# One gemv unit ahead of the last mean matmuls and four or five behind, at three entries of a two-block transformer kernel

## The chip, the core and the metric

The kernel runs on one core of a Trainium2 chip. The metric is the device time of one execution in microseconds, as the median of several runs. One execution was also profiled; rows below are from its trace. PE is TensorE's matmul side and PEld its weight loads, DVE is VectorE, ACT ScalarE, POOL GpSimd and SP the engine whose queue issues the weight transfers.

## What is computed

Two transformer blocks over one sequence of 256 tokens, 1024 channels wide, in float32. The first block has two layers, each with a mixer and a SwiGLU FFN; between them one key/value product is made from the residual stream:

```
h = x
for layer in range(2):
    sh1, sc1, g1, sh2, sc2, g2 = split(silu(c) @ mod_w[layer] + mod_b[layer], 6)
    u = rms_norm(h, norm_mix) * (1 + sc1) + sh1
    h = h + g1 * (hgrn2(u) if layer == 0 else band_attention(u, k, v))
    u = rms_norm(h, norm_ffn) * (1 + sc2) + sh2
    h = h + g2 * swiglu(u, ffn_w_in, ffn_w_out)
    if layer == 0:
        shift, scale = split(silu(c) @ kv_mod_w + kv_mod_b, 2)
        k, v = split((rms_norm(h, kv_norm) * (1 + scale) + shift) @ kv_w, 2)
x = rms_norm(h, final_norm)
```

The second block has four kinds of attention side by side and a convolutional FFN; the diff does not touch its code.

## The kernel before

Activations lie transposed (channels on partitions). Every product in full precision is made of three fp32r matmuls (mm3, lines 258 to 260): weights and activations are each split into a rounded high part and a low remainder. A weight arrives as a *unit* of 512 KB: `emit_dma` (L186) loads it into one of 7 raw buffers (RAW_BUFS), `emit_conv` casts it on ACT (w_hi, L193) and subtracts on DVE (w_lo, L195) into one of 4 pairs of buffers. A raw buffer is free again when its unit has been converted.

The modulation vectors are products of one row with a matrix (gemv). Their units are *raw*: not converted, but multiplied in float32 straight from the raw buffer, on PE with the row as weights (L524) or on DVE by multiply and add (L516, L518). A raw buffer of such a unit is free when the engine has read it. `gemv` has 8 units; `gemv_x` does the first 5 (NF) on PE and the rest on DVE.

The program is a list of steps, and the instructions are emitted step by step, for all engines, in that order. Before each step `pump` emits what may be emitted of transfers and conversions: the transfer of unit i if unit i-7 has been consumed in an earlier step, and the conversion of the next weight unit j if at most 2 (AHEAD) converted units lie ahead and `j <= state["pos"] + state["look"]`, where pos is the number of units that the steps so far have taken, raw ones included. look is 4 (LOOK) from the first projections on.

There are three *entries* where a product begins on a freshly normalized residual: the FFN of layer 0 (stA), the key/value product (stB) and the FFN of layer 1 (stC). The product before each (the last step of an output projection or of an FFN) works on four banks of 512 columns; after each bank DVE adds into the residual (L623), ACT squares (L428) and PE sums the squares with a matrix of constants (`stat_mm`, L463), each time one bank or more behind. `barrier` lays out the rest: gemv units in `fill`, and in a step f between them the last mean matmul, ACT's logarithm and exponential (L468, L469) and `apply_parts`: for each of 8 channel groups a scaled product on DVE (nt, L573), the high part on ACT (s, L579) and the low part on DVE (s, L585). The next product's first matmul needs the first high part. For stB and stC, fill is the first 5 units of a gemv_x product (g12, g15). For stA it is part of the 8 units of the sixth modulation product of layer 0 (g05), all on PE; three of these 8 stand ahead of the last step of the output projection (`aproj[6:]`, which takes two weight units).

Of the kernel before, what the change touches and what calls it, by code (L numbers as in the profile page):

```python
# [27 lines left out]
NF = 5  # L28
NG = 6
LOOK = 4  # L30
NB = 2
RAW_BUFS = 7
WT_BUFS = 4
AHEAD = 2
# [14 lines left out]
HG_ORDER = """  # L49
# [82 lines left out]
def kernel(ctx: ExitStack, tc: tile.TileContext, x, c, mod_w, mod_b, norm_mix, norm_ffn,  # L132
# [28 lines left out]
    def open_phase(name):  # L161
        if "cm" in phase:
            phase["cm"].__exit__(None, None, None)
        phase["cm"] = tc.tile_pool(name=name, bufs=2, reuse_waits="tile")
        phase["p"] = phase["cm"].__enter__()

    def ph(w, name, bufs=2, dt=F32, tag=None):
        return phase["p"].tile([P, w], dt, name=name, tag=tag or name, bufs=bufs)
# [9 lines left out]
    state = {"pos": 0, "dma": 0, "conv": 0, "conv_w": 0, "used_w": 0, "look": -1, "late": None}  # L178
# [123 lines left out]
    def out_proj(w, ks, operand, evac, nlast=2):  # L302
        box = {}

        def first(i, u):
            if i == 0:
                box["a"] = [acc_bank() for _ in range(4)]
            hi, lo = operand(ks[i])
            acc_pairs(box["a"], u, hi, lo, range(4), i == 0, False)

        n0 = len(ks) - nlast

        def last(*us):
            for j in range(4):
                for i, u in enumerate(us, n0):
                    hi, lo = operand(ks[i])
                    acc_pairs(box["a"], u, hi, lo, [j], False, i == len(ks) - 1)
                evac(j, box["a"][j])

        st = [Step(lambda u, i=i: first(i, u), [unit_row(w, P * ks[i])], 2.6) for i in range(n0)]  # L320
        st.append(Step(last, [unit_row(w, P * k) for k in ks[n0:]], 2.6 * nlast))
        return st
# [143 lines left out]
    def rstd_of(st, w=256, name="rstd", bufs=2):  # L466
        r = small(512, name, bufs)[:, :w]
        SC.activation(r, st, AF.Ln, bias=epsc, scale=1.0)  # L468
        SC.activation(r, r, AF.Exp, scale=-0.5)  # L469
        return r  # L470
# [31 lines left out]
    def gemv(w, c0, dst, bias, on_pe=KT, tags=("ga", "ga")):  # L502

        box = {}

        def acc(k, u):
            if k == 0 and on_pe:
                box["g"] = bank("gv", 1)
            if k < on_pe:
                total(crep[:, k, :], u.raw[:, 0, :], k == 0, k == KT - 1)  # L510
                return
            if k == on_pe:
                box["a"] = [ph(512, t, 2) for t in tags]
            for a, w_ in zip(box["a"], (u.raw[:, 0, 0:512], u.raw[:, 0, 512:D])):
                if k == on_pe:
                    DV.tensor_scalar(a, w_, ca[:, k:k + 1], None, op0=OP.mult)  # L516
                else:
                    DV.scalar_tensor_tensor(a, w_, ca[:, k:k + 1], a, op0=OP.mult, op1=OP.add)  # L518

        def total(by, rows, start, stop):  # L520
            g = box["g"]
            for j in range(4):
                r = rows[:, 256 * j:256 * j + 256] if rows is not None else box["a"][j // 2][:, 256 * (j % 2):256 * (j % 2) + 256]
                PE.matmul(g[32 * j:32 * j + 32, 0:256], lhsT=by, rhs=r, start=start, stop=stop, tile_position=(0, 32 * j))  # L524
            if stop:
                box["s"] = small(256, "gsb", 2)
                SC.copy(box["s"], g[:, 0:256])

        def rest():
            if not on_pe:  # L530
                box["g"] = bank()
            total(ones, None, not on_pe, True)

        st = [Step(lambda u, k=k: acc(k, u), [unit_gemv(w, P * k, c0)], 0.5) for k in range(KT)]
        st += [Step(rest, [], 0.1)] if on_pe < KT else []
        return st + [Step(lambda: gemv_fin(box["s"], dst, bias), [], 0.5 if on_pe == KT else 0.1)]
# [10 lines left out]
    def gemv_mod(layer, i, gemv=gemv):  # L547
        return gemv(mod_w[layer], D * i, modT[layer][:, 8 * i:8 * i + 8], modb[layer][:, 8 * i:8 * i + 8])

    def mod(layer, i):  # L550
        return modT[layer][:, 8 * i:8 * i + 8]

    def a_col(dst, gain, sc):
        DV.scalar_tensor_tensor(dst, sc, 1.0, gain, op0=OP.add, op1=OP.mult)
# [3 lines left out]
    def apply(*args):  # L558
        for _ in apply_parts(*args):
            pass  # L560
# [28 lines left out]
    def act(tag):  # L589
        return lambda: ubox[tag]  # L590

    def stat_lag(j, stats):
        for i in ((), (), (0,), (1, 2), (3,))[j]:
            for st in stats:
                stat_mm(st["p"], st[i], i)

    def barrier(stat, first, then, fill):


        def f():  # L600
            stat_lag(4, [stat])
            first()
            stat["r"] = rstd_of(stat["p"][:, 0:256])
            then()
        return fill[:NB] + [Step(f)] + fill[NB:]

# [12 lines left out]
    def residual(gate, stat, tables=False):  # L619
        def evac(j, p):  # L620
            for m in range(2):
                k = 2 * j + m
                DV.scalar_tensor_tensor(hT()[:, k], p[:, 256 * m:256 * m + 256], gate()[:, k:k + 1], hT()[:, k],  # L623
                                        op0=OP.mult, op1=OP.add)
            sq = square(hT()[:, 2 * j:2 * j + 2].rearrange("p k t -> p (k t)"))
            if j == 0:
                stat["p"] = bank()
                if tables:
                    exp_tables()
            stat[j] = sq  # L630
            stat_lag(j, [stat])
        return evac

    steps = []
# [143 lines left out]
    items = {}  # L778
# [200 lines left out]
    def ordered(items, order, name):  # L979
        order = order.split()  # L980
        assert sorted(order) == sorted(items), set(order) ^ set(items)
        return [s for key in order for s in items[key]]

    def S_(f, *a, cost=1.0):
        return Step(lambda: f(*a), [], cost)
# [17 lines left out]
    for n in range(8):  # L1003
        items[f"v{n}"] = v_steps[n:n + 1]
    stA = {}
    aproj = out_proj(a_w_out[0], list(range(KT)), lambda k: tuple(OP_[k // 2, "o"][i][:, S * (k % 2):S * (k % 2) + S] for i in (2, 0)),
                     residual(lambda: mod(0, 2), stA))
    for n in range(6):
        items[f"a{n}"] = aproj[n:n + 1]
    for i in (2, 3, 4):  # L1010
# [4 lines left out]
            items[f"q{i}"] = g[8:-1]  # L1015
        items[f"z{i}"] = g[-1:]
    g05 = gemv_mod(0, 5)
    steps += [Step(exp_tables), Step(lambda: SY.dma_start(late, t_late))]
    steps += ordered(items, HG_ORDER, "hg") + g05[:8 - NF] + aproj[6:]

    def apply_ffn(tag, slots, layer, stat, off_col):
        A = cols[:, off_col:off_col + 8]

        def first():
            if layer == 0:
                open_phase("mid")
                A_["flip"] = ph(P, "flip", 1, F32R)
                DV.tensor_copy(A_["flip"], flip)
            a_col(A, nffn[layer], mod(layer, 4))

        return first, lambda: apply(tag, slots, A, mod(layer, 3), stat["r"])
# [53 lines left out]
    def down_T_last(evac):  # L1085
        def f(acc, us, h):
            for j in range(4):
                for i in range(2):
                    acc_pairs(acc, us[i], h[0][:, i], h[1][:, i], [j], False, i == 1)
                evac(j, acc[j])  # L1090
        return f
# [2 lines left out]
    A_ = {}  # L1094
    kv_gemv = [gemv_v(kv_mod_w, D * i, kvmodT[:, 8 * i:8 * i + 8], vcol("kv_mod_b")[:, 8 * i:8 * i + 8])
               for i in range(2)]
    steps += barrier(stA, *apply_ffn("f0", (1, 2), 0, stA, 32), g05[8 - NF:8])

    def unit_bias(i):
        rb = b_rel_bias[0]  # L1100
# [4 lines left out]
    def bias_turn(i, u):  # L1105
# [4 lines left out]
        for s in range(2):  # L1110
            b = bank()
            for w in (u.hi, u.lo):
# [7 lines left out]
    f0 = ffn(ffn_w_in[0], 0, ffn_w_in[0], FFN, ffn_w_out[0], R0, act("f0"), swi_gate, mul_hidden, down_T,  # L1120
             down_T_last(residual(lambda: mod(0, 5), stB, True)))
# [149 lines left out]
    items = {}  # L1271
# [570 lines left out]
    items = {"sca": [Step(b2_scale)], "col": [Step(b2_cols)], "cx": [S_(c_x)]}  # L1842
# [55 lines left out]
```

## Time and profile before

| | us |
|---|---|
| median of 3 runs | 1136.26 (1135.9 to 1138.14) |
| the profiled execution | 1137.38 |
| its span, first to last instruction | 1135.6 |
| PE busy | 1098.3 (97%) |
| DVE busy | 763.1 (67%) |
| ACT busy | 572.9 (50%) |
| mean granted TensorE clock | 0.996 |

Rows of a timeline are: start, length, engine, line, operation, output and inputs with shapes, count, and in brackets the idle time of the engine just ahead with what ended it. Rows with a count above 1 merge neighbours of one kind. The granted clock is 1.00 at 2.4 GHz and 0.50 at 1.2 GHz.

### The profile page before, as it was taken

Reading aid. Unit: us, or ns where it says so; the run is one execution under the profiler, and the core shown is the slowest. Engines: PE = TensorE matmul, PEld = TensorE weight load, DVE = VectorE, ACT = ScalarE, POOL = GpSimd, SP = SyncE. Lnnn points to the kernel's source line nnn. Section 1 sums busy time; section 2 is a strip of 40 time slices with the busy share of each in tenths; the row PEclk is TensorE's granted clock in tenths of the full one; section 3 lists DMA queues with packets and bytes.
Section 4 is the critical chain, followed back from the end, with each engine's and each line's share of the span. In section 5 each row is a group of like instructions: output and inputs, shape, how many; then the busy total and the mean of one; then the engine's idle time right before and its main releaser. Section 6 shows DMA issues by size and latency. Waiting matters only on the chain.

```text
span 1135.6 us, 23604 instructions
## 1 busy us (share of the span) xinstructions
PE 1098.3 (97%) x9689; PEld 1014.6 (89%) x9689; DVE 763.1 (67%) x1237; ACT 572.9 (50%) x913; POOL 141.7 (12%) x201
## 2 busy tenths in 40 slices
PE   6899999999999999999999999999989999999997
PEld 4887888999999978788999999988879999999997
DVE  3577885777677598776555455677766766666676
ACT  2456464543444565655444344646655454454454
POOL 4044410000000001240000000024322110010010
PEclk9999999999999999999999999999998999999999
DMA  9976687898998597865765565873342655655651
GB/s 275 297 256 233 220 272 236 289 311 273 303 303 274 199 294 232 272 225 191 225 213 186 186 203 148 171 196 122 112 148 89 216 179 186 196 175 186 197 175 56
DMA packets 176124, 241.92 MB, mean 213 GB/s; under 512 B 18712, under 2 KB 142160, under 8 KB 176016
## 3 DMA queue, kind: packets, MB, share of 16 engines
q1 hardware_dynamic: 174928, 239.54, 66.8%
q8 instruction: 76, 1.25, 0.4%
q0 software_dynamic: 912, 0.81, 0.4%
q14 instruction: 32, 0.26, 0.1%
q10 hardware_dynamic: 176, 0.07, 0.0%
HBM read 239.33 MB, written 1.05 MB: 212 GB/s over the span
## 4 chain that ended last, share of the span: by engine, by line
PE 84%; DVE 5%; ACT 4%; DMA 3%; POOL 2%; issue 1%; SPq 0%; DVEq 0%; ACTq 0%; POOLq 0%
PE pb_b L258 15%; PE pb_b L260 15%; PE pb_b L259 14%; PE pb_acc L258 11%; PE pb_acc L260 10%; PE pb_acc L259 10%; DMA w_raw<-in_a_w_in_dram 2%; ACT w_hi L193 2%; DVE w_lo L195 2%; PE pb_b L463 1%; POOL dp L860 1%; PE pb_gv L524 1%; PE pb_b L1222 1%; DVE nt L573 1%; DMA w_raw<-in_mod_w_dram 1%
## 5 line engine op out<-in xcount | busy, mean ns | idle before, releaser
L195 DVE TENSOR_TENSOR w_lo<-w_raw,w_hi 128x1024 fp32r<-128x1024 f32 (+1 forms) x335 | 408.4, 1243 | 165.4 <-ACT w_hi L193 164.8
L258 PE MATMUL pb_b<-s,w_hi 128*128 128x256 f32 x1488 | 420.3, 282 | 5.3 <-ACT s L1756 2.9
L260 PE MATMUL pb_b<-s,w_lo 128*128 128x256 f32 x1488 | 417.4, 281 | 1.6 <-DVE w_lo L195 1.5
L259 PE MATMUL pb_b<-s,w_hi 128*128 128x256 f32 x1488 | 417.8, 281 | 0.3
L193 ACT CAST w_hi<-w_raw 128x1024 fp32r<-128x1024 f32 (+1 forms) x336 | 342.2, 1044 | 88.7 <-DMA w_raw<-in_a_w_in_dram 23.5
L258 PEld LDWEIGHTS pb_b<-s,w_hi 128*128 128x128 f32 x1488 | 281.0, 189 | 12.8 <-issue 4.0
L260 PEld LDWEIGHTS pb_b<-s,w_lo 128*128 128x128 f32 x1488 | 280.9, 189 | 2.5 <-DVE w_lo L195 2.4
L259 PEld LDWEIGHTS pb_b<-s,w_hi 128*128 128x128 f32 x1488 | 281.0, 189 | 1.9 <-DVE s L585 0.7
L258 PE MATMUL pb_acc<-s,w_hi 128*128 128x256 f32 x720 | 205.2, 285 | 1.8 <-ACT w_hi L193 1.7
L260 PE MATMUL pb_acc<-s,w_lo 128*128 128x256 f32 x720 | 201.5, 280 | 2.6 <-DVE w_lo L195 2.6
L259 PE MATMUL pb_acc<-s,w_hi 128*128 128x256 f32 x720 | 201.0, 279 | 0.1
L258 PEld LDWEIGHTS pb_acc<-s,w_hi 128*128 128x128 f32 x720 | 135.3, 188 | 9.2 <-issue 5.0
L260 PEld LDWEIGHTS pb_acc<-s,w_lo 128*128 128x128 f32 x720 | 135.3, 188 | 3.4 <-DVE w_lo L195 3.4
L259 PEld LDWEIGHTS pb_acc<-s,w_hi 128*128 128x128 f32 x720 | 135.4, 188 | 0.5 <-DVE s L585 0.3
L1215 POOL TENSOR_SCALAR att<-att,sm 128x128 f32<-128x128 f32 (+1 forms) x72 | 46.0, 657 | 617.4 <-DVE sm L1208 338.5
L1069 ACT CAST s<-sig 128x512 fp32r<-128x512 f32 x38 | 23.6, 621 | 117.6 <-DVE sig L1079 117.6
L258 PE MATMUL pb_acc<-w_hi,s 128*128 128x512 f32 x192 | 77.5, 404 | 1.4 <-ACT s L579 1.0
L259 PE MATMUL pb_acc<-w_lo,s 128*128 128x512 f32 x192 | 76.0, 396 | 0.8 <-DVE w_lo L195 0.8
L260 PE MATMUL pb_acc<-w_hi,s 128*128 128x512 f32 x192 | 76.1, 396 | 0.0
L1782 ACT ACTIVATE sig<-att,vb_t,vc_t 128x256 f32<-128x256 f32 x32 | 17.5, 594 | 75.4 <-DVE att L1777 75.4
L1792 POOL TENSOR_TENSOR sig<-sig,rstd 128x512 f32<-128x512 f32 x16 | 22.7, 1422 | 238.6 <-ACT sig L1790 238.6
L1075 ACT ACTIVATE sig<-pb_b 128x512 f32<-128x512 f32 x22 | 13.2, 598 | 75.1 <-PE pb_b L260 75.1
(367 smaller groups left out, 1166.6 us busy)
## 6 DMA issues: line engine op xcount, KB each, us to landing
w_raw<-in_mod_w_dram SPq DMA_DIRECT2D x96, 512.0 KB, 5.2
w_raw<-in_ffn_w_in_dram SPq DMA_DIRECT2D x88, 512.0 KB, 5.3
w_raw<-in_ffn_w_out_dram SPq DMA_DIRECT2D x44, 512.0 KB, 4.8
w_raw<-in_a_w_in_dram SPq DMA_DIRECT2D x32, 512.0 KB, 6.1
w_raw<-in_ffn_w_gate_dram SPq DMA_DIRECT2D x32, 512.0 KB, 3.7
w_raw<-in_ffn_w_up_dram SPq DMA_DIRECT2D x32, 512.0 KB, 5.4
w_raw<-in_ffn_w_down_dram SPq DMA_DIRECT2D x32, 512.0 KB, 3.5
w_raw<-in_kv_mod_w_dram SPq DMA_DIRECT2D x16, 512.0 KB, 5.6
```

Source lines behind the costliest of these rows:

```text
L193: SC.copy(hi, raw)
L195: DV.tensor_sub(lo, raw, hi.bitcast(F32))
L258: PE.matmul(o, lhsT=whi, rhs=xhi, start=start, stop=False, skip_group_check=True)
L259: PE.matmul(o, lhsT=whi, rhs=xlo, start=False, stop=False, skip_group_check=True)
L260: PE.matmul(o, lhsT=wlo, rhs=xhi, start=False, stop=stop, skip_group_check=True)
L463: PE.matmul(st[:, 0:256], lhsT=mean_d, rhs=sq[:, 256 * m:256 * m + 256], start=j == 0 and m == 0, stop=j == n - 1 and m == 1)
L524: PE.matmul(g[32 * j:32 * j + 32, 0:256], lhsT=by, rhs=r, start=start, stop=stop, tile_position=(0, 32 * j))
L1069: SC.copy(hi, hid)
L1075: SC.activation(sg, g, AF.Silu)
L1215: GP.tensor_scalar(t[:, i, cs], t[:, i, cs], r[:, 2 * b + i:2 * b + i + 1], 1.0, op0=OP.mult, op1=OP.mult)
L1782: SC.activation(zm, am, AF.Identity, bias=vcol("conv_b")[:, f:f + 1], scale=vc_t[:, 64 + f:65 + f])
L1792: GP.tensor_mul(zp, zp, rs_pair())
```

## The change

NB, the number of units of `fill` ahead of step f, goes from 2 to 1; g05 keeps two units, not three, ahead of the last projection step, so that 1 stands ahead of f and 5 behind at stA, and 1 and 4 at stB and stC (before: 2 and 3). look becomes 6 in front of the first entry and 5 behind it, and stays 5.

```diff
-NB = 2
+NB = 1
...
     g05 = gemv_mod(0, 5)
+    look_on = Step(lambda: state.update(look=7 - NB))
     steps += [Step(exp_tables), Step(lambda: SY.dma_start(late, t_late))]
-    steps += ordered(items, HG_ORDER, "hg") + g05[:8 - NF] + aproj[6:]
+    steps += ordered(items, HG_ORDER, "hg") + g05[:7 - NF] + aproj[6:] + [look_on]
...
-    steps += barrier(stA, *apply_ffn("f0", (1, 2), 0, stA, 32), g05[8 - NF:8])
+    steps += barrier(stA, *apply_ffn("f0", (1, 2), 0, stA, 32), g05[7 - NF:8])
+    steps.append(Step(lambda: state.update(look=6 - NB)))
```

The step in which f lies between the parts of fill is unchanged:

```
    return fill[:NB] + [Step(f)] + fill[NB:]
```

## Rows read from the trace of the kernel before

**Rows 1.** The page's first part: busy time, share and instructions of PE.
```profile
PE 1098.3 (97%) x9689; PEld 1014.6 (89%) x9689; DVE 763.1 (67%) x1237; ACT 572.9 (50%) x913; POOL 141.7 (12%) x201
```

**Rows 2.** The timeline around the first entry, 193 to 207 us.
```profile
193.25 0.63 ACT L428 ACTIVATE sq<-s 128x512 f32<-128x512 f32 x1 [1.65 <-DVE s L623]
193.78 1.98 ACT L193 CAST w_hi<-w_raw 128x1024 fp32r<-128x1024 f32 x2
...
193.88 1.07 PE L524 MATMUL pb_gv<-w_raw,crep 128*32 128x256 f32 x16
194.84 2.36 DVE L195 TENSOR_TENSOR w_lo<-w_raw,w_hi 128x1024 fp32r<-128x1024 f32 x2 [1.71 <-ACT w_hi L193]
...
194.88 1.13 PE L463 MATMUL pb_b<-sq,early 128*128 128x256 f32 x4
...
195.94 1.50 PE L524 MATMUL pb_gv<-w_raw,crep 128*32 128x256 f32 x24
196.04 0.47 ACT L468 ACTIVATE rstd<-pb_b,epsc 128x256 f32<-128x256 f32 x1 [0.29 <-PE pb_b L463]
...
196.55 0.42 ACT L469 ACTIVATE rstd<-rstd 128x256 f32<-128x256 f32 x1
...
197.54 0.88 DVE L573 SCALAR_TENSOR_TENSOR nt<-s,cols,rstd 128x256 f32<-128x256 f32 x2
...
198.62 0.38 PE L258 MATMUL pb_b<-s,w_hi 128*128 128x256 f32 x1 [1.18 <-ACT s L579]
...
206.24 0.38 PE L260 MATMUL pb_b<-s,w_lo 128*128 128x256 f32 x1 [0.56 <-DVE w_lo L195]
```

**Rows 3.** The timeline at the third entry.
```profile
521.89 2.36 DVE L195 TENSOR_TENSOR w_lo<-w_raw,w_hi 128x1024 fp32r<-128x1024 f32 x2 [1.71 <-ACT w_hi L193]
...
524.44 0.88 DVE L573 SCALAR_TENSOR_TENSOR nt<-s,cols,rstd 128x256 f32<-128x256 f32 x2
```

**Rows 4.** The timeline of SP's queue at the first entry: issues of FFN weights.
```profile
185.19 0.93 SPq L186 DMA_DIRECT2D w_raw<-in_ffn_w_in_dram  x2
...
194.58 0.37 SPq L186 DMA_DIRECT2D w_raw<-in_ffn_w_in_dram  x1
```

**Rows 5.** Busy time by stage: stretch, length, engines, clock, DMA share, GB/s.
```profile
192.00:195.30 3.30, 3.30 (x28) 2.20 (x28) 1.33 (x3) 2.05 (x3) 0.00 (x0) 1.00 0.02 4
```

**Rows 6.** DMA issues from 194 to 194.8: count, KB, us to landing.
```profile
w_raw<-in_ffn_w_in_dram SPq DMA_DIRECT2D x1, 512.0 KB, 3.7
```

**Rows 7.** The timeline of PE where the second block's FFN begins.
```profile
851.23 0.58 PE L258 MATMUL pb_b<-s,w_hi 128*128 128x256 f32 x1 [2.88 <-ACT s L1756]
```

**Rows 8.** Busy time by stage, as in rows 5: the last three columns begin with the clock.
```profile
195.30:206.50 11.20, 9.32 (x80) 7.61 (x79) 10.26 (x22) 7.83 (x15) 0.00 (x0) 1.00 0.95 320
...
851.00:857.00 6.00, 5.77 (x25) 5.54 (x26) 5.44 (x12) 3.53 (x8) 5.66 (x7) 0.50 0.13 53
```

**Rows 9.** The timeline behind the key/value entry, 410 to 419 us.
```profile
410.14 0.88 DVE L516 TENSOR_SCALAR ga<-w_raw,ca 128x512 f32<-128x512 f32 x2
...
410.31 1.06 ACT L193 CAST w_hi<-w_raw 128x1024 fp32r<-128x1024 f32 x1 [1.34 <-DMA w_raw<-in_kv_w_dram]
...
411.39 1.23 DVE L195 TENSOR_TENSOR w_lo<-w_raw,w_hi 128x1024 fp32r<-128x1024 f32 x1 [0.38 <-ACT w_hi L193]
...
417.17 1.22 DVE L195 TENSOR_TENSOR w_lo<-w_raw,w_hi 128x1024 fp32r<-128x1024 f32 x1
...
418.44 0.38 PE L260 MATMUL pb_b<-s,w_lo 128*128 128x256 f32 x1
```

**Rows 10.** The timeline of the attention's first pairs, 442 to 449 us.
```profile
442.68 3.23 POOL L1215 TENSOR_SCALAR att<-att,sm 128x128 f32<-128x128 f32 x8 [283.59 <-DVE sm L1208]
...
443.79 0.17 DVE L1208 RECIPROCAL sm<-sm 128x4 f32<-128x4 f32 x1
...
445.12 2.19 ACT L193 CAST w_hi<-w_raw 128x1024 fp32r<-128x1024 f32 x2
...
448.59 0.82 PE L1222 MATMUL pb_b<-early,att 128*128 128x128 f32 x6
```

## The prediction

> **What bounds the kernel now.** I read the page first, then the waits of PE, then the order of time around the three places that the diff touches, then the SP queue and the transfers there. PE is busy 97% of the span [rows 1], so a change pays only where PE stands still, and costs wherever it makes PE stand still. At each FFN entry and at the key/value product PE does stand still: 1.18 us before the first matmul of the first FFN [rows 2].
>
> What ends that wait is not what the gemv units suggest. In [rows 2] ACT squares the last pair at 193.25, then casts two weight units (W0 and W1, the two halves of the first gate product) until 195.76, and only then, at 196.04, takes the logarithm of the mean. The exponential is done at 196.97, yet the first scaled product (nt, L573) starts on DVE at 197.54: DVE is still subtracting for W0 and W1 (L195) until 197.20. The first matmul follows the first nt by 1.08 us. So the chain is: square, cast W0, cast W1, low part of W1, nt, matmul. PE's mean matmul (194.88 to 196.01) and its gemv units lie beside it. The third place repeats this: low parts from 521.89 to 524.25, nt at 524.44 [rows 3]; so does the second.
>
> **The change, part by part.** *One unit ahead instead of two, at the second and third place.* The unit ahead covers the time from the last projection matmul to the last square; two units take 1.07 us and three take 1.50, so one unit is 0.43 us [rows 2]. The square is ready at 193.88, as the first unit starts, so one unit suffices. The mean matmul moves up by 0.43 us and the logarithm by at most 0.28 us, until ACT's casts end. But nt waits for DVE's low parts, and neither their order nor that of the casts changes: I walked pump's two conditions (consumed, look) over the order of units, with NB 2 and look 4, and with NB 1 and the new looks. W0 and W1 are still converted between the square and the logarithm. Gain 0; the cover that hides it is the low part of W1. If it were gone, the gain would be up to 0.43 us at each place.
>
> *The first place: a unit moved from before the last projection step to behind it.* Here the same walk gives something else. Name the eight units of the sixth modulation product G0 to G7. Before: G0 to G2, the last projection step, G3, G4, mean matmul, G5 to G7. After: G0, G1, last step, G2, mean matmul, G3 to G7. There are seven raw buffers. Before, once the last step's own units are converted, they hold G3 to G7, W0 and W1: both weights are issued at 185.19 [rows 4] and have long landed when their casts start at 193.78. DMA is idle by then, 2% from 192 to 195.3 [rows 5]. After, six gemv units wait, G2 to G7, and the seventh buffer is W0's. W1 has no buffer until G2 is consumed, behind the last projection step. With look 6, pump still emits the cast of W1 ahead of the barrier step, so on ACT it stands in front of the logarithm and on DVE in front of nt, and each engine takes its instructions in the order in which they are emitted.
>
> The price: today W2 (first half of the up product) is in the same position. Its buffer is G3's; G3 starts at 193.88 [rows 2], the transfer is issued at 194.58 [rows 4] and lands 3.7 us later [rows 6], on idle DMA. G2 will run where G3 did, less the 0.43 us of the unit that no longer precedes the last step: W1 is issued at 194.15 and lands at 197.85. Its cast takes 1.03 us (half of the pair, with the overlap), to about 198.93. The logarithm then starts 2.9 us later than now and the exponential ends near 199.85. DVE's low part, 1.22 us, runs to 200.17; nt follows as now after 0.34, at 200.51, and the first matmul 1.08 us later, near 201.6 instead of 198.62: **+3.0 us**. PE's work up to there is the same, so it ends at 197.44 as now and the wait grows from 1.18 to about 4.1 us. Late next is all of the first apply and then W2's cast, which keep their distance from it. Below: without the stall the moved unit alone would give 0.4 us back. Above: if the allocator gives W1 the buffer of W0, which is free only after W0's low part (195.6), the transfer starts 1.5 us later, so +4.5. I take +3.0, since W2 is the same transfer under the same conditions. The later transfers move from G3, G4... to half a microsecond to one later each, and their casts move by 3 us, so none of them becomes late.
>
> *TensorE's clock.* A wait of 2.88 us ends at 851.23 [rows 7], and behind it the granted clock is 0.50 (1.2 GHz) for the 6 us from 851 to 857, with 25 matmuls, 0.24 us each [rows 8]. The 1.18 us wait left it at 1.0 (195.3 to 206.5). A 4.1 us wait will very likely drop it. The first two weight units are 48 matmuls and today take 6.6 us, because DVE delivers the operands (198.62 to the wait that ends at 206.24, which is another 0.56 us on a low part [rows 2]). With some 5 to 6.5 us of them at 0.24 us and the rest at the full rate of about 0.12 us, they end 0.5 to 1.5 us past the point where that low part would be ready: **+1.0 us**; 0 if the clock holds. The Trainium skill (TensorE: Matmul & The Clock Gate, Part 1) says that the low level is the default and that activity lifts it, so a stall would be paid a second time in slow matmuls; by that the first place costs 4.0 us, without it 3.0. The row at 851 agrees with it.
>
> *The look of 5 that stays for the rest of the kernel.* It matters only where raw gemv units stand between weights, so by the same walk it changes nothing in either first-block FFN or in the second block, but in the attention layer about a dozen conversions move up by one step. The first is behind the key/value entry: the conversion of the third key weight is now emitted before the first gemv unit on DVE instead of after it. Its cast waits 1.34 us for its transfer until 410.31 [rows 9]. Today DVE uses that wait for the gemv pair (410.14, 0.88 us for two, about 0.8 of DVE's time); after, DVE waits for the cast, takes the low part at 411.39 and only then the gemv pair. DVE is then full up to the low part at 417.17, which ends at 418.39, and PE's first matmul on it starts at 418.44: no slack. **+0.9 us** (0 if the transfer lands sooner; up to 1.5, because the buffer of the second gemv unit is now freed behind the mean matmul and the transfers of this entry queue up behind it). In the rest, for instance, a low part now stands before the reciprocal at 443.79: its cast is one of the pair from 445.12, so the reciprocal slips to about 447.4, POOL needs some 1.6 us (eight scalings took 3.23), and the transposes that run at 448.59 [rows 10] slip by half a microsecond. Others meet slack. **+0.3 us**, between 0 and 1.5. A gain is bounded by the waits that are there, under 1 us in that stage.
>
> **Sum.** 3.0 + 1.0 + 0.9 + 0.3 = +5.2 us. The profiled run took 1137.38 us (span 1135.6 and 1.8 around it), 1.1 above the median of 1136.26; on its own scale it becomes 1142.6, and from the median 1141.4.
>
> **The rivals.** (a) *No change.* The stall does not arise, because W1 finds a buffer in time or its cast falls behind the logarithm; then 0.4 us are gained at the first place and 0 to 1.5 lost at the attention: 1135.9 to 1137.4. For it: nothing else in the three entries changes. Against: seven buffers, and eight units wanted. A change of 0.2%, 2.3 us, is about what a measurement of this kernel can tell. (b) *Faster.* The logarithm, not the low parts, sets the end, so that an earlier mean matmul closes PE's waits at all three places: at most three times 1.18, or 3.5 us, 1132.7; it decides only if nt starts at the end of the exponential. Against: it starts 0.57 us behind it [rows 2]. (c) *A stall without the rest:* the first place costs 3.0, the clock holds and the attention absorbs the shifts: 1139.2. (d) *Everything high:* 4.5 + 1.5 + 1.5 + 1.5: 1145.3.
>
> **How the numbers follow.** The forecast with its neighbours (c) and (d) has 0.82 (of it (c) 0.2, (d) 0.06), (a) 0.13, (b) 0.05. The forecast's own range is 1139 to 1143.8. Leaving out (b), most of (a) and the end of (d) gives 1137.8 to 1143.8. Slower by over 0.2% 0.82, within 0.13, faster 0.05.
>
> **What would show it.** Right: at the first FFN the second cast waits on a transfer from ffn_w_in for about 3 us; the logarithm starts near 199; PE's first matmul waits about 4 us for s (L579); a clock of 0.5 behind it; nt at the other two entries as far behind the low parts as now. At 410 the gemv pair follows the low part, and PE waits near 418 on a low part. Wrong: no DMA wait of that cast, or a logarithm ahead of it; then (a). A first wait as said but a total under +2 would mean that time came back later, in the attention's earlier conversions.

## The result and the profile after

The changed kernel takes 1144.64 us (median of 6 runs, 1142.0 to 1149.46); the kernel before, run beside it, 1136.95 (6 runs, 1135.9 to 1138.83). The ratio is 1.0064, with a 95% interval of 1.0042 to 1.0086: slower by about 7.3 us, between 4.8 and 9.8. The forecast was 1141.4 in a range of 1137.8 to 1143.8, so the direction was right and the time lies 0.84 us above the range. The profiled execution of the changed kernel took 1143.04 us with a span of 1141.3, 5.7 more than the span before.

First the page's busy times of the changed kernel, which answer to [rows 1]:

```profile
PE 1099.9 (96%) x9689; PEld 1016.5 (89%) x9689; DVE 763.1 (67%) x1237; ACT 572.9 (50%) x913; POOL 142.0 (12%) x201
```

The instruction counts are the same. PE is busy 1.6 us longer, which goes with the stretches of low clock shown below; the rest of the 5.7 us is waiting. The timeline of the changed kernel at the first entry answers to [rows 2] and [rows 4]:

```profile
191.20 0.63 ACT L428 ACTIVATE sq<-s 128x512 f32<-128x512 f32 x1 [1.66 <-DVE s L623]
191.73 1.03 ACT L193 CAST w_hi<-w_raw 128x1024 fp32r<-128x1024 f32 x1
191.82 0.64 PE L524 MATMUL pb_gv<-w_raw,crep 128*32 128x256 f32 x8
...
192.39 1.13 PE L463 MATMUL pb_b<-sq,early 128*128 128x256 f32 x4
192.52 2.00 SPq L186 DMA_DIRECT2D w_raw<-in_ffn_w_in_dram  x2
192.79 1.23 DVE L195 TENSOR_TENSOR w_lo<-w_raw,w_hi 128x1024 fp32r<-128x1024 f32 x1 [1.71 <-ACT w_hi L193]
...
193.45 2.37 PE L524 MATMUL pb_gv<-w_raw,crep 128*32 128x256 f32 x40
...
196.09 1.04 ACT L193 CAST w_hi<-w_raw 128x1024 fp32r<-128x1024 f32 x1 [3.33 <-DMA w_raw<-in_ffn_w_in_dram]
...
197.04 0.47 ACT L468 ACTIVATE rstd<-pb_b,epsc 128x256 f32<-128x256 f32 x1
197.16 1.23 DVE L195 TENSOR_TENSOR w_lo<-w_raw,w_hi 128x1024 fp32r<-128x1024 f32 x1 [3.15 <-ACT w_hi L193]
...
198.72 0.88 DVE L573 SCALAR_TENSOR_TENSOR nt<-s,cols,rstd 128x256 f32<-128x256 f32 x2
...
199.80 0.43 PE L258 MATMUL pb_b<-s,w_hi 128*128 128x256 f32 x1 [3.98 <-ACT s L579]
```

The second cast (W1) waits 3.33 us for its transfer, which SP issues when the gemv unit that starts at 191.82 has been read. The logarithm and nt stand behind that cast and its low part, and the first product matmul waits 3.98 us instead of 1.18. From the last square to the first matmul it is 8.60 us; before it was 5.37 [rows 2].

At the key/value entry, ACT, DVE and PE of the changed kernel, to be set against [rows 9]:

```profile
408.75 1.04 ACT L193 CAST w_hi<-w_raw 128x1024 fp32r<-128x1024 f32 x1 [0.70 <-DMA w_raw<-in_kv_w_dram]
410.24 1.04 ACT L193 CAST w_hi<-w_raw 128x1024 fp32r<-128x1024 f32 x1 [0.44 <-DMA w_raw<-in_kv_w_dram]
...
412.84 1.22 DVE L195 TENSOR_TENSOR w_lo<-w_raw,w_hi 128x1024 fp32r<-128x1024 f32 x1 [0.26 <-ACT w_hi L193]
413.98 0.88 DVE L516 TENSOR_SCALAR ga<-w_raw,ca 128x512 f32<-128x512 f32 x2
```

```profile
409.85 0.50 PE L258 MATMUL pb_acc<-w_hi,s 128*128 128x512 f32 x1 [1.16 <-ACT w_hi L193]
411.11 0.50 PE L259 MATMUL pb_acc<-w_lo,s 128*128 128x512 f32 x1 [0.76 <-DVE w_lo L195]
```

The gemv pair on DVE now stands behind the low part, as the prediction said. But what PE waits for is earlier: the third weight unit of this product (v2 below) lands late and its cast waits 0.70 us for it. PE's waits in this stretch, for the kernel before:

```profile
PE pb_acc L258 <- ACT s L579: 1.0, 1, 1.0
PE pb_acc L259 <- DVE w_lo L195: 0.8, 1, 0.8
PE pb_acc L258 <- ACT w_hi L193: 0.4, 1, 0.4
```

Only the last of the three changed, from 0.4 to 1.16 us. SP's queue shows that v2's transfer starts later: its issues of key/value weights, v2's first, in the kernel before and below it in the changed one:

```profile
399.64 2.54 SPq L186 DMA_DIRECT2D w_raw<-in_kv_w_dram  x4
```

```profile
401.32 3.67 SPq L186 DMA_DIRECT2D w_raw<-in_kv_w_dram  x4
```

The changed execution is 1.2 us behind here (table below), so v2's transfer is issued 0.5 us later against the rest. Two places ahead of it in the queue stands a transfer into the buffer of the second gemv unit, which PE now reads behind the mean matmul; that one goes from 398.02 to 400.41, 1.2 us more than the shift.

Then the attention of the changed kernel (DVE, POOL, and PE at the transposes of the second head pair), to be set against [rows 10]:

```profile
449.19 1.23 DVE L195 TENSOR_TENSOR w_lo<-w_raw,w_hi 128x1024 fp32r<-128x1024 f32 x1 [1.95 <-ACT w_hi L193]
450.33 0.17 DVE L1210 RECIPROCAL sm<-sm 128x4 f32<-128x4 f32 x1
450.42 0.53 DVE L1226 COPY pt<-pb_b 128x384 f32<-128x384 f32 x1
450.86 1.41 DVE L518 SCALAR_TENSOR_TENSOR ga<-w_raw,ca,ga 128x512 f32<-128x512 f32 x2
452.19 1.22 DVE L195 TENSOR_TENSOR w_lo<-w_raw,w_hi 128x1024 fp32r<-128x1024 f32 x1
```

```profile
446.03 1.63 POOL L1217 TENSOR_SCALAR att<-att,sm 128x128 f32<-128x128 f32 x4 [288.61 <-DVE sm L1210]
450.67 4.66 POOL L1217 TENSOR_SCALAR att<-att,sm 128x128 f32<-128x128 f32 x4 [3.01 <-ACT w_hi L193]
```

```profile
454.50 0.55 PE L1224 MATMUL pb_b<-early,att 128*128 128x128 f32 x3 [2.29 <-POOL att L1217]
455.38 0.44 PE L1224 MATMUL pb_b<-early,att 128*128 128x128 f32 x2 [0.34 <-POOL att L1217]
```

The reciprocal (L1210; L1208 before) waits behind a low part, as forecast. POOL's four scalings then take 4.66 us, where the four of the pair before took 1.63, and PE stands still for 2.29 us.

Behind each of the three places the granted clock fell. Busy time by stage for those stretches (the last three columns are clock, DMA share and GB/s):

```profile
199.90:203.40 3.50, 3.41 (x15) 3.17 (x16) 3.50 (x10) 2.11 (x5) 0.00 (x0) 0.51 1.08 380
...
411.60:415.00 3.40, 3.40 (x10) 2.67 (x9) 3.14 (x5) 1.46 (x2) 0.00 (x0) 0.50 0.84 242
...
456.00:459.40 3.40, 3.40 (x18) 3.40 (x17) 3.37 (x9) 1.05 (x1) 0.00 (x0) 0.50 1.01 340
```

The account of the whole span comes from the start of the same product matmul (L258) in both traces. The shift is after less before; steps at the first entry, at the key/value entry and in the attention are the change's as far as the experiments below bear them out, the others are not (both kernels are the same up to 185 us, and in the second block):

```
matmul at (before)   shift    step and what it is
  62 to 185          -1.7     the two executions differ at the start
 206.46              +1.2     +2.9  first entry: W1 has no buffer
 407.85              +2.0     +0.8  key/value: v2 lands late
 411.78              +3.5     +1.5  clock 0.50 from 411.6 to 415.0
 449.59              +6.0     +2.4  transposes wait for POOL
 451.80              +7.4     +1.4  clock 0.50 from 456.0 to 459.4
 483.45              +7.7     +0.3
 633.42              +6.7     -1.0  540 to 635: the trace of before is one of five that are slower here
 857.46              +5.7     -1.0  second block: 6.8 us of low clock before, 3.4 after
```

So the change costs 2.9 + 2.3 + 4.1 = 9.3 us in these two executions, and 7.3 us (4.8 to 9.8) by the ratio of the timed runs. Steps of this size also come without any change: with the code of before, the clock fell at 107 to 109 us in three of the traces below (look_only, one_conv, scale_dve) and cost 1.5 us each time.

### The profile page after: what moved, and what is told of

Same layout as the page of the kernel before. It is cut to its first block, busy times and chain, and to the rows that moved or that the text cites. A ratio compares the mean times of both kernels' runs of the same rounds, so it can differ in the third digit from the quotient of the medians.

```text
span 1141.3 us, 23605 instructions
## 1 busy us (share of the span) xinstructions
PE 1099.9 (96%) x9689; PEld 1016.5 (89%) x9689; DVE 763.1 (67%) x1237; ACT 572.9 (50%) x913; POOL 142.0 (12%) x201
## 4 chain that ended last, share of the span: by engine, by line
PE 85%; DMA 4%; DVE 4%; ACT 3%; POOL 2%; issue 1%; SPq 0%; DVEq 0%; ACTq 0%; POOLq 0%
PE pb_b L258 15%; PE pb_b L259 15%; PE pb_b L260 15%; PE pb_acc L258 11%; PE pb_acc L260 10%; PE pb_acc L259 10%; DMA w_raw<-in_a_w_in_dram 2%; PE pb_b L463 2%; DVE w_lo L195 2%; ACT w_hi L193 2%; PE pb_gv L524 1%; POOL dp L860 1%; PE pb_b L1224 1%; DMA w_raw<-in_mod_w_dram 1%; POOL att L1217 1%
## 5 line engine op out<-in xcount | busy, mean ns | idle before, releaser
L258 PE MATMUL pb_b<-s,w_hi 128*128 128x256 f32 x1488 | 420.9, 283 | 7.9 <-ACT s L579 5.0
L258 PEld LDWEIGHTS pb_b<-s,w_hi 128*128 128x128 f32 x1488 | 281.8, 189 | 15.2 <-ACT s L579 6.4
L258 PE MATMUL pb_acc<-s,w_hi 128*128 128x256 f32 x720 | 205.2, 285 | 0.1
L258 PEld LDWEIGHTS pb_acc<-s,w_hi 128*128 128x128 f32 x720 | 135.3, 188 | 7.3 <-issue 5.2
L258 PE MATMUL pb_acc<-w_hi,s 128*128 128x512 f32 x192 | 78.2, 407 | 2.2 <-ACT w_hi L193 1.2
```

What stands on the lines that cost most here:

```text
L258: PE.matmul(o, lhsT=whi, rhs=xhi, start=start, stop=False, skip_group_check=True)
```

## The experiments

Each kernel is timed against the kernel before on the same chip, in five rounds. Where a shift is named, it is read as in the account above.

**look_back: is it the look that stays at 5?** The change with look put back to 4 right behind f at every entry:

```diff
-        return fill[:NB] + [Step(f)] + fill[NB:]
+        return fill[:NB] + [Step(f), Step(lambda: state.update(look=4))] + fill[NB:]
...
-    steps.append(Step(lambda: state.update(look=6 - NB)))
...
+    steps.append(Step(lambda: state.update(look=5)))
```

The last line stands ahead of the key/value and the third entry. In first_only, kv_only, one_ahead_ac and the kernels named early, barrier takes NB as an argument, 2 where none is given, and sets look to 4 behind f.

> The change with look set back to 4 right behind each of the three entries, so that the conversions in the attention layer stand where they stood before. Theory 1 (separate prices: the first entry loses about 2.9 us for want of a raw buffer, and the look of 5 in the attention layer loses about 4 us by moving a low part ahead of a reciprocal): 2.9 us at the first entry, up to 0.8 us at the key/value entry where the transfers start later (2.3 if the clock falls there), nothing in the attention: 3 to 5 us over the kernel before. Theory 2 (the stall at the first entry shifts transfers and engines against each other, and the attention loses because of that shift): 7 us over before, with the transposes still waiting 2 us for POOL.

1144.2 us, ratio 1.0051 (1.0034 to 1.0068), or +5.8 us (3.9 to 7.7), over the 3 to 5 expected. The attention lost nothing: the shift goes from 8.7 to 8.4 between 419 and 518 us, and PE does not wait for POOL. The first entry cost +3.0 again and, with the clock low for 6.8 us (201.8 to 208.6) instead of 3.4, +1.3 more. The key/value entry cost +2.5 and +1.5 of clock, though the conversion behind it stands as before. Of PE's three waits there, one is longer:

```profile
PE pb_acc L258 <- ACT w_hi L193: 2.8, 1, 2.8
```

So the loss of the attention belongs to the look, and that of the key/value entry does not. What was saved in the attention this execution lost at the entries; by the totals alone look_back could not be told from the change.

**look_only: the look alone.** The kernel before, with one step behind the first entry:

```diff
+    steps.append(Step(lambda: state.update(look=5)))
```

> The kernel before, with two units ahead as it was, but look 5 from behind the first entry on. Theory 1: no stall at the first entry; PE waits over 2 us for POOL at the second pair of transposes of the attention, and the clock falls behind it or at the key/value entry: 3.5 to 6 us over before. Theory 2: 0 to 1 us over before.

1144.08 us, ratio 1.0062 (1.0039 to 1.0085). The first entry is as before. The attention costs +2.2 and +1.3 of clock, so those are the look's. The key/value entry costs +0.6 ahead of the matmul at 407.85, which kernels with nothing changed there reach too (see kv_only). The surprise is the third entry, +3.3 (and a clock of 0.50 from 536.0 to 539.4, of which the apply chain hid all but 0.2). With two gemv units ahead, a look of 5 reaches one weight unit further there, and it has no buffer; that is the stall of the first entry again, at another place and with the other setting. ACT, and PE's waits:

```profile
531.54 1.04 ACT L193 CAST w_hi<-w_raw 128x1024 fp32r<-128x1024 f32 x1 [2.39 <-DMA w_raw<-in_ffn_w_in_dram]
```

```profile
PE pb_b L258 <- ACT s L579: 4.3, 1, 4.3
```

**first_only: the first entry alone.** Its units and look as in the change, look 4 behind f, the rest as before:

```diff
+    look_on = Step(lambda: state.update(look=6))
...
+    steps += ordered(items, HG_ORDER, "hg") + g05[:7 - NF] + aproj[6:] + [look_on]
...
+    steps += barrier(stA, *apply_ffn("f0", (1, 2), 0, stA, 32), g05[7 - NF:8], 1)
```

> The first entry alone as in the change (two units ahead of the last projection step, one ahead of the mean matmul, five behind, look 6 up to there and 4 behind); the other two entries and look as before. Theory 1: the second cast waits about 3.3 us for its transfer and PE about 4 us for its first matmul; 2.9 us over before, and nothing later. Theory 2: 6 to 7 us over before, with the waits in the attention.

1140.07 us, ratio 1.002 (1.0008 to 1.0033), or +2.3 us (0.9 to 3.8); in the trace +3.0 at the first entry. The clock was 0.50 from 199.8 to 203.2 and that cost nothing: PE falls 1.1 us further behind by the matmul at 201.86, and at 206.46, where the kernel before waits 0.56 us for a low part [rows 2], it has made that up. The stall is a loss by itself.

**room: one unit ahead, but a buffer for W1.** The change with three gemv units ahead of the last projection step, as before, and four behind f. One unit more has then been taken, so look is 5, not 6, ahead of the first entry to reach the same weight:

```diff
-    look_on = Step(lambda: state.update(look=7 - NB))
+    look_on = Step(lambda: state.update(look=6 - NB))
...
-    steps += ordered(items, HG_ORDER, "hg") + g05[:7 - NF] + aproj[6:] + [look_on]
+    steps += ordered(items, HG_ORDER, "hg") + g05[:8 - NF] + aproj[6:] + [look_on]
```

> The change, but with three units ahead of the last projection step as before, so one ahead and four behind at the first entry and a raw buffer for the second weight unit; look 5 from there on. Theory 1: no transfer wait of the second cast, first matmul of the FFN as far behind the last square as before (5.4 us), so 0 at the first entry; what remains is the look of 5 and the key/value entry, 4 to 5 us over before. Theory 3 (one unit ahead is too little work for PE, or the square is not ready): the first entry still loses 2 us or more, 7 us over before.

1143.66 us, ratio 1.0054 (1.0034 to 1.0074). The stall of the first entry is gone, and nothing is gained there either; PE's waits in that stretch are those of before. The rest came back: +1.7 and +1.4 at the key/value entry, +2.75, +1.5 and +0.6 in the attention. It tells that the missing buffer causes the stall. Its total, +6.1 us (3.9 to 8.4), cannot be told from the change's 7.3; in this execution PE's wait for v2 was 2.1 us.

**kv_only: the key/value entry alone.** One unit ahead and four behind there, look 5 for the entry only:

```diff
+    steps.append(Step(lambda: state.update(look=5)))
+    steps += barrier(stB, kv_cols, kv_start, g12[:NF], 1)
```

> The kernel before with one unit ahead and four behind at the key/value entry alone, look 5 for that entry and 4 right behind it. Theory 1 (the second gemv unit is read behind the mean matmul, so its buffer and all transfers behind it come later while DMA is the limit): the casts of the key/value weights wait for their transfers, PE's first matmul on the third value weight is 1 to 2.5 us later against the entry's start; 1 to 2.5 us over before, up to 4 if the clock falls. Rival (one unit ahead costs nothing here, the lateness came from the look of 5): 0.

1140.46 us, ratio 1.0024 (1.0009 to 1.0039), or +2.7 us. In the trace the shift goes from -1.5 to +0.9 there, 1.0 of it ahead of the matmul at 407.85, the rest under a clock of 0.50 (408.2 to 411.7). ACT of this kernel:

```profile
406.26 1.04 ACT L193 CAST w_hi<-w_raw 128x1024 fp32r<-128x1024 f32 x1 [0.87 <-DMA w_raw<-in_kv_w_dram]
407.99 1.05 ACT L193 CAST w_hi<-w_raw 128x1024 fp32r<-128x1024 f32 x1 [0.69 <-DMA w_raw<-in_kv_w_dram]
409.51 1.05 ACT L193 CAST w_hi<-w_raw 128x1024 fp32r<-128x1024 f32 x1 [0.48 <-DMA w_raw<-in_kv_w_dram]
```

Three casts in a row wait for transfers. That alone is no sign of the change: they do so too in low_behind and scale_dve, whose key/value entry is that of before. What the change moves is the issue. With each execution's shift at the entry taken off, v2's transfer is issued at 399.6 us in all ten traces with two units ahead (early_abc 399.5) and at 400.1 in all four with one (the change, look_back, room, kv_only). From issue to landing it takes 6.6 to 7.7 us in the ten and 7.4 to 9.1 in the four. PE then waits 0.3 to 1.0 us for v2 in the ten and 1.2 to 2.8 in the four, and the step ahead of the matmul at 407.85 is 0 to 0.7 us against 0.8 to 2.5. The clock fell there in all four, and in one of the ten (scale_dve, 412.3 to 415.7, after a wait of 1.0 us).

**one_conv: one conversion of the attention.** The kernel before, with a look of 5 for the one step ahead of the second pair's scaling (fi1), so that the third query weight (qa2) is converted ahead of it:

```diff
+    items["v3"].append(Step(lambda: state.update(look=5)))
+    items["fi1"].insert(0, Step(lambda: state.update(look=4)))
```

> The kernel before with a single conversion moved up by one step: in the attention layer the low part of one query weight now stands ahead of the reciprocal of the second pair and not behind the copy of the first. Theory 1 (this one conversion carries the attention's loss, because the reciprocal waits for a cast and POOL's four scalings then run beside busy DVE work): PE waits over 2 us for POOL at the second pair of transposes, 2.5 us over before, 4 with a fall of the clock. Rival (the loss is spread over the dozen conversions): under 1 us over before.

1140.2 us, ratio 1.0027 (1.0014 to 1.004), or +3.1 us for one moved conversion. The trace has the same picture as the changed kernel: low part 445.99, reciprocal 447.13, POOL 4.58 us, PE waiting 1.15 and 1.39 us, and the clock at 0.50 from 452.1 to 455.5; the shift goes from +0.1 to +2.8 and to +4.2. Of the dozen conversions that a look of 5 moves, this one makes nearly all of the loss of the attention (2.4 + 1.4 in the changed kernel). The clock fell at this place in the four traces that have this conversion early and POOL at work on the scalings (the change, look_only, room, one_conv), and in none of the other ten.

**low_behind: the cast moved, the low part not.** one_conv with the low part of qa2 behind the reciprocal; the order on DVE differs in this one pair, and that of all other engines not at all. cast_next emits the cast of the next weight unit and holds its low part back, and low_next emits that:

```diff
+    items["fi1"].insert(0, Step(cast_next))
+    items["fi1"].append(Step(low_next))
```

> The kernel before with the conversion of the first weight of the third query product moved ahead of the scaling of the second head pair, as in one_conv, but its low part (DVE) put behind the reciprocal of that pair, where one_conv has it ahead; its cast stays where one_conv has it, and so do ACT's, POOL's, SP's and PE's orders. Theory (the reciprocal waits behind the low part, and all of the loss hangs on that): the four scalings end before 446, PE does not wait at the pair's transposes, time within 0.5 us of the kernel before, against the +3.1 us of one_conv. Rival (the cast that is now ahead of ACT's copy and exponentials, or the raw buffer that comes free earlier, does the harm): still +2 us or more. A part of each: +1 us.

1137.08 us beside 1136.55, ratio 1.0008 (0.9993 to 1.0023); the shift changes by less than 0.25 us between 408 and 510 us. DVE and POOL of this kernel:

```profile
446.43 0.17 DVE L1231 RECIPROCAL sm<-sm 128x4 f32<-128x4 f32 x1
448.48 1.22 DVE L242 TENSOR_TENSOR w_lo<-w_raw,w_hi 128x1024 fp32r<-128x1024 f32 x1 [1.89 <-ACT w_hi L194]
```

```profile
445.68 2.88 POOL L1238 TENSOR_SCALAR att<-att,sm 128x128 f32<-128x128 f32 x7
```

The reciprocal runs 2 us ahead of the low part, in the time in which DVE waits for the cast, and the scalings take 0.41 us each. The cast ahead of it on ACT does no harm. The loss hangs on two DVE instructions changing places.

**scale_dve: the late reciprocal, without POOL.** one_conv with the four scalings of that pair on DVE:

```diff
-        scale_rows(t, softmax_inv(s))
+        scale_rows(t, softmax_inv(s), DV if p == 1 else None)
```

> one_conv with the four scalings of the second head pair on DVE, right behind the reciprocal, in place of POOL. The reciprocal stays as late as in one_conv, about 3.3 us later than before; only POOL's four scalings (4.58 us there beside DVE's low parts and multiply-adds, 1.6 us elsewhere) are gone. Theory (the slip of the reciprocal is the smaller half, POOL's pace beside a busy DVE the larger): the scalings end by 448.7 on the scale of one_conv, the transposes start there at the latest, PE waits under 0.5 us and the clock stays up: +0.3 us against the kernel before, with 1.1 us more work on DVE that could make it +1. Rival (the slip of the reciprocal alone makes the loss): PE waits 1.5 us or more and the time is +2 to +3 us, as in one_conv.

1137.17 us beside 1136.55, ratio 1.0008 (0.9995 to 1.002); PE does not wait at those transposes, and the shift is +3.7 ahead of the attention and +3.4 behind it. (That execution was late before it came to the changed code: the clock fell at 108.5 and at 412.3 us.) DVE of this kernel:

```profile
449.35 1.23 DVE L195 TENSOR_TENSOR w_lo<-w_raw,w_hi 128x1024 fp32r<-128x1024 f32 x1 [1.95 <-ACT w_hi L193]
450.49 0.17 DVE L1208 RECIPROCAL sm<-sm 128x4 f32<-128x4 f32 x1
450.69 1.01 DVE L1215 TENSOR_SCALAR att<-att,sm 128x128 f32<-128x128 f32 x4
```

The reciprocal is as late as in one_conv, and that alone costs nothing. It is the slip and POOL's pace together: after the slip the scalings fall into a stretch of low parts and multiply-adds on DVE. The scalings of one_conv and, below it, the eight of the kernel before (min, median and max of one, in ns):

```profile
L1215 POOL TENSOR_SCALAR att<-att,sm x4: 371/1156/1956, 447.5 to 450.1; 128x128 f32<-128x128 f32 x2, 128x256 f32<-128x256 f32 x2
```

```profile
L1215 POOL TENSOR_SCALAR att<-att,sm x8: 363/424/475, 442.7 to 445.4; 128x128 f32<-128x128 f32 x4, 128x256 f32<-128x256 f32 x4
```

**one_ahead_ac: the idea without its side effects.** One gemv unit ahead of f at the first and third entry, three ahead of the last projection step so that W1 has its buffer, two ahead at the key/value entry, look 5 ahead of the two entries and 4 behind each f:

```diff
+    steps += ordered(items, HG_ORDER, "hg") + g05[:8 - NF] + aproj[6:] + [Step(lambda: state.update(look=5))]
...
+    steps += barrier(stA, *apply_ffn("f0", (1, 2), 0, stA, 32), g05[8 - NF:8], 1)
...
+    steps.append(Step(lambda: state.update(look=5)))
+    steps += barrier(stC, *apply_ffn("f1", (1, 2), 1, stC, 56), g15[:NF], 1)
```

> One unit ahead and four behind at the first and third entry, with three units ahead of the last projection step as before (so the second weight has its buffer), two ahead at the key/value entry, look 5 for each of the two entries and 4 behind them. Theory 1 (nt waits for DVE's low parts, not for the logarithm): 0, within 0.5 us of before, with nt starting as far behind the last square as before. Rival (the earlier mean matmul pays): 0.8 us or more under before.

1138.68 us beside 1137.09, ratio 1.001 (0.9997 to 1.0023): no difference that can be told. In the trace the first product matmul waits 1.17 us (1.18 before). Last square and nt:

```profile
192.74 0.63 ACT L428 ACTIVATE sq<-s 128x512 f32<-128x512 f32 x1 [1.65 <-DVE s L623]
```

```profile
197.03 0.88 DVE L573 SCALAR_TENSOR_TENSOR nt<-s,cols,rstd 128x256 f32<-128x256 f32 x2
```

From square to nt it is 4.29 us, exactly as in [rows 2] (193.25 to 197.54), although the mean matmul came earlier. What the change moves does not set the start of the product.

**early_ac: what does set it.** As one_ahead_ac, with the cast of W0 emitted ahead of the last square and its low part right behind the last residual addition, at the first and third entry:

```diff
+    def out_proj(w, ks, operand, evac, nlast=2, ahead=False):
...
+                if ahead and j == 2:
+                    cast_next()
+            if ahead:
+                low_next()
```

> As one_ahead_ac, and the cast of the first weight unit of the FFN is emitted ahead of the last square and its low part behind the last residual addition, at the first and third entry. Theory 1 (the low parts are what nt waits for): the first matmul of each of the two FFNs comes about 1 us earlier against the last square, 2 us under before. Rival (the wait then moves to the weight's transfer or to the late square): 0 to 2 us over before.

1135.63 us beside 1137.09, ratio 0.9991 (0.998 to 1.0003); run again beside other kernels (early_ac_2) 1136.26 beside 1136.55, ratio 0.9997 (0.9982 to 1.0011).

> The kernel of early_ac once more, on the chip of these runs. If its gain is real: 1 to 2 us below the kernel before, with an interval that stays below 1.0. If it was noise: within 0.5 us, on either side.

By the trace the step works: from the last square to nt 3.33 us instead of 4.29, and PE's first wait falls from 1.18 to 0.2 us:

```profile
192.92 0.63 ACT L455 ACTIVATE sq<-s 128x512 f32<-128x512 f32 x1 [0.71 <-DVE s L650]
...
196.25 0.88 DVE L600 SCALAR_TENSOR_TENSOR nt<-s,cols,rstd 128x256 f32<-128x256 f32 x2 [0.29 <-ACT rstd L496]
197.33 0.39 PE L281 MATMUL pb_b<-s,w_hi 128*128 128x256 f32 x1 [0.21 <-ACT s L606]
```

Now nt does wait for the exponential (L496). Both traces show the step, 1.0 us at the first entry and 0.8 at the third. That is less than these runs can tell from nothing in the total, and of the first run's gain the second showed little.

**early_abc: the same at all three.** The early cast at the key/value entry too, with two units ahead there.

> early_ac with the same change at the key/value entry (two units ahead there): the cast of the first weight unit ahead of the last square, its low part behind the last residual addition. If the chain square, cast, cast, low part sets the start of the product there too, the first matmul comes about 0.9 us earlier and the time is 0.9 us below early_ac. If the transfers of that entry set the pace (the third weight unit lands late already), the 0.9 us come back as a longer wait for it: same as early_ac within 0.4 us.

1134.88 us beside 1136.55, ratio 0.9982 (0.9968 to 0.9995), or 2.0 us faster (0.6 to 3.6): the one kernel of these that is faster than the kernel before with an interval below 1, and only just. In the trace the shift falls by 1.0 at the first entry, 0.4 at the key/value entry and 0.8 at the third; the key/value entry gives less than half of the 0.9 that was hoped for. Whether the early cast would do the same with two units ahead was not run. PE's waits at the key/value entry, where the third unit's cast still costs 0.3:

```profile
PE pb_acc L282 <- DVE w_lo L196: 0.8, 1, 0.8
PE pb_acc L281 <- ACT s L606: 0.6, 1, 0.6
PE pb_acc L281 <- ACT w_hi L194: 0.3, 1, 0.3
```

## Where the prediction was right, and the step that failed

**One unit ahead brings nothing at the second and third place, +0.** Right for the start of the product: one_ahead_ac keeps the 4.29 us from square to nt with one unit ahead (read at the first entry), and the early cast, not the early mean, shortens it. At the third entry the changed kernel's shift does not move (7.7 ahead of it and behind). At the key/value entry the one unit ahead had a cost all the same, by the late transfer below.

**The first entry, +3.0 by a missing buffer.** Right in each step: the cast waits 3.33 us for its transfer, the logarithm and nt come after it, PE waits 3.98 us (about 4.1 forecast), and the shift is +2.9. first_only shows it alone (+2.3, 0.9 to 3.8), and room takes it away with the buffer.

**The clock behind it, +1.0.** The clock fell, but the cost was 0 in the changed kernel's trace (3.4 us low, where the prediction had 5 to 6.5) and 1.3 in look_back's (6.8 us low). DVE paces this stretch, so a short fall is made up (first_only). The Trainium skill (TensorE: Matmul & The Clock Gate, Part 1) has the low level as the default that activity lifts; the trace agrees, with a clock of 0.51 behind the 3.98 us wait. What it added to the time was 0 to 1.3 us.

**The key/value entry, +0.9 by DVE's order.** The order is as forecast, but it is not what costs: the shift is 3.5 us ahead of the matmul at 418 and 3.4 behind it, and the wait on a low part that was to show there did not come. The cost is the late transfer, which the prediction had only as the upper bound of this term: PE's wait for v2 went from 0.4 to 1.16 us, and to 2.8 us in look_back, where DVE's order is the old one. With the clock's fall behind it, which the prediction did not count here, the term is 2.3 us; kv_only gives 2.7 (1.0 to 4.4). So this term was mis-sized too, and by a wrong mechanism.

**The step that failed: the rest of the attention, +0.3 us (0 to 1.5).** It measured 4.1. The prediction had found the very instruction, the reciprocal that slips behind a low part, but it priced POOL's four scalings at 1.6 us from rows in which DVE was on short work or idle, and so let the transposes slip by half a microsecond. They took 4.66 us beside DVE's low parts and multiply-adds, and PE's 2.29 us wait brought the clock down once more, +1.4, which the prediction did not count here either. A row of the kernel before shows the price, for a pair where PE did not have to wait for it, and the prediction does not use it (the timeline of POOL there):

```profile
455.20 4.81 POOL L1215 TENSOR_SCALAR att<-att,sm 128x128 f32<-128x128 f32 x4 [9.29 <-DVE sm L1208]
```

There DVE works on multiply-adds and low parts from 454.96 to 458.61, and the first of the four scalings alone takes 3.56 us. low_behind and scale_dve show the mechanism from both sides: put the reciprocal back ahead of the low part, or take POOL out of it, and the loss is gone. The Trainium skill (SBUF — State Buffer, Who interferes with whom) states that a DVE instruction with two SBUF inputs contends with a GpSimd instruction that reads SBUF; the low part and the multiply-add are of that kind. The durations here agree: a scaling of 0.36 to 0.48 us beside other DVE work took 3.56 us beside a run of these. That contention of this kind, and nothing else of a busy DVE, is what slows POOL is the Trainium skill's account; no run here takes it apart.

So the terms measured 2.9, 0, 2.3 and 4.1 for 3.0, 1.0, 0.9 and 0.3. The timed runs of the three parts alone agree with this account: first_only 2.3, kv_only 2.7 and one_conv 3.1 us make 8.1, beside the change's 7.3 (4.8 to 9.8). Of the rivals, (a) and (b) fell: the stall came, with a buffer nothing was gained (room), and the early mean closes no wait. (c) fell too, since the attention did not absorb the shifts. (d) was nearest in total, but put the loss in other places.

**Open.** The issue of v2's transfer moves by 0.5 us, always by the same; why the transfer then takes 7.4 us in one execution and 9.1 in another is not shown, so the size of the key/value term is not settled. Also not settled is why five traces (before, look_back, kv_only, one_ahead_ac, early_ac) run 0.8 to 1.0 us slower than the other nine between 540 and 635 us; the kernels' differences do not sort them.

## What to carry to other kernels

A global look-ahead that is raised for one place moves work at every other place: the look made the largest loss here, some 250 us behind the place it was raised for, and one swap of two DVE instructions was most of it. With as many raw buffers as waiting units, a unit that is held back withholds a buffer, and an in-order engine that stands at the cast of the weight without one holds all that is queued behind it. Before giving a matmul an earlier slot, find the chain that ends last: here it was the casts and low parts between the last square and the first product. Moving one cast ahead at each entry shortened the entries by 1.0, 0.4 and 0.8 us (2.0 in the total, 0.6 to 3.6) where moving the mean alone gave nothing.

## What the runs showed of the hardware

POOL's scaling of 128x128 or 128x256 elements takes 0.42 us in the median beside short or no DVE work, and 1.16 us, up to 1.96, beside DVE's low parts and multiply-adds (one_conv; 2.55 for one in the changed kernel and 3.56 in the kernel before); on DVE the four took 1.01 us together (scale_dve).

The granted clock fell to 0.50 behind waits of PE of 2.29 and 0.34 us in the attention, and at the key/value entry in a stretch with three waits of 1.0, 1.16 and 0.76 us; with 1.0, 1.0 and 0.8 us it fell too (scale_dve); with 1.0, 0.4 and 0.8 us, as before, and with 1.0, 0.9 and 0.8 us (look_only) it stayed up. It stayed low for 3.4 us in most falls and 6.8 us in some: behind the first entry's wait of 4.0 to 4.1 us, 3.4 us in two kernels (the change, first_only) and 6.8 in a third (look_back). Each fall cost between 0 and 1.6 us, by whether PE was the engine that the stretch waited for.

v2's transfer of 512 KB, the fourth of seven that are issued within 5 us, took 6.6 to 9.1 us from issue to landing; one that met idle DMA at the first entry took 3.7 [rows 5, rows 6].
